# A four-layer decoder trunk on one Trainium2 core: later turns, own banks, a twelfth warming product, one division for a pair of heads

## The chip, the cores and the metric

The kernel runs on one core of one Trainium2 chip. The metric is the time of one execution in device microseconds; three runs of the kernel before gave a median of 1155.39 us. The core has five engines, each with its own queue of instructions: TensorE (PE in the profile; its weight loads are shown apart as PEld), VectorE (DVE), ScalarE (ACT), GpSimd (POOL) and SyncE (SP), which here issues the DMAs. An instruction starts when those ahead of it on its engine are issued and the semaphores that it waits for are up.

## What is computed

One sequence of 256 tokens, 1024 wide, goes through four layers. Each is a token mixer behind an RMS norm, added to the residual stream, and a squared-ReLU MLP (4096 wide) behind another norm. The mixers are differential attention (layers 0 and 3), MoBA block attention (layer 1, one block of 256 here, so plain causal attention) and sliding-window attention with attention sinks (SWA, layer 2). Cut to what matters here:

```python
x = x + mixer[i % 3](rms_norm(x, g_mix), ...)
x = x + relu(rms_norm(x, g_mlp) @ w_up) ** 2 @ w_down
# diff (8 heads, value width 128):  p = softmax(q0 k0) - lam * softmax(q1 k1)
#                                   o = rms_norm(p @ v, sub_g) * (1 - lambda_init)
# MoBA and SWA (16 heads of 64):    p = exp(s - m) / l ;  o = p @ v
# SWA: only the last 128 keys count, and l = sum(exp(s - m)) + exp(sink - m)
out = rms_norm(x, final_g)
```

Products are to have float32 accuracy. The kernel splits each operand in two parts (hi and lo, type fp32r) and adds three products: hi with hi, hi with lo, lo with hi.

## The kernel before

**Weights.** The weights come as pieces of 1 MB. SP's queue fetches them five ahead (`fetch`, L57 to L69, into `raw`), ACT makes the hi part (`whi`, L80) and DVE the lo part (`wlo`, L81), two pieces ahead of their use. This goes on all the time beside everything else that ACT and DVE do.

**Layout.** The residual stream lies transposed in four tiles `hT` of 128x512. Projections (`proj`, tile `p_in`, L296) take 24 products for each of the two tiles of 128 tokens, 512 columns wide, or 256 in SWA (two pairs of heads); between the two halves of 24, the steps named `midway` are issued. The output projection (`p_d`, L271 to L273 in `mm3`) adds to four PSUM banks held through the whole of it.

**Order.** The kernel text is written as one stream; a scheduler then orders the instructions of each engine, keeping close to the text and to what is ready. Two sets of four PSUM banks rotate: "wk" (p_s0, p_s1, p_t, p_av, p_qk, p_o and the like) and "acc" (p_in, p_d, p_down, p_last). A tile that gets a bank waits for the last reader of the tile that had it.

**Heads of 64 (MoBA, SWA).** `head_block` (L415) handles two heads at once, as a generator with three steps. First `scores` (L313): TensorE makes p_s0 and p_s1, DVE adds the mask and takes the minimum of the negated scores (L333), ACT exponentiates (L336) and sums the row into `l`; SWA adds the sink's term (L340, L341). Then the division: DVE makes the reciprocal (L420) and multiplies head 0 with two tensor_scalars (L426), ACT does head 1 with two copies with a scale (L424). Second `transposed` (L346): TensorE transposes the numerators `e` (three p_t for each head, L351), ACT copies them out (`et`, L352). Third the products with the values, p_av (L434), for the two heads in one bank, each in its own 64 columns of TensorE, and the copies out as hi and lo (`oo`, L437 and L438).

In SWA, `step` (L443) keeps up to three such blocks in flight: a new block is appended, then every block in the line is given its next step, second-oldest first up to the newest, and the oldest last when there are more than three. There are four projections (`for c in range(4)`) with two blocks each; the first of them starts with p_qk, the transposes of the queries (L459), and `put_q` (`qhl`, L468 and L469). MoBA and the diff layers follow a plan written out by hand (L567 to L574): for each half of a projection a list of steps, QK (turned queries and keys), SC (scores), TR (transposed), AV (values), OUT (results).

**Diff layers.** `diff_pair` (L391) takes two heads: the values' products, the norm of each head (a reciprocal root `ry`), `o` on DVE (L404), four transposes p_o on TensorE (L409), and `oo` as hi on ACT (L411) and lo on DVE (L412). OUT(g) is the step that issues p_o and what follows for pair g. OUT(1) stands with TR(4) and AV(4) between the two halves of a projection; OUT(3) is the last step of the plan, and `out_proj_all` (L627) comes after it: four groups g of weights, eight blocks d of the output, six products for each, and group g needs `oo` of pair g.

**The tail.** `down_out` (L691) makes the last MLP's second product the other way round (p_last, tokens on the partitions), for two halves c of 512 columns and two tiles t of 128 tokens. `close` (L699) adds a bank to the residual with DVE (L702) and squares it with ACT (L704, the sum goes to `fss`); `finish` (L706) makes the reciprocal root (L710 to L717), scales the first half with ACT (L719) and the second with DVE (L722), and sends the result out. The very last tile's columns are made in two halves of 256 that share a bank: the first half is closed, then the second.

**The start.** WARM (L31) products of a tile of ones (p_warm, L133) run before the first data are there.

## Time and profile before

| | us |
|---|---|
| median of three runs (lowest, highest) | 1155.39 (1154.45, 1156.26) |
| the profiled execution, its own time | 1154.87 |
| its span, from the first to the last instruction | 1152.8 |
| of that the MoBA mixer's stretch, 308 to 421 | 113.0 |
| the SWA mixer's stretch, 600.86 to 671.83 | 70.97 |
| from the start of the last product (1145.27) to the end of the span | 7.5 |

The mean granted clock of TensorE is 0.998. The profile's groups give an instruction's line, engine, operation, output and inputs with their shapes, how often it occurs, its busy time and mean length in ns, and the idle time ahead of it with what ended it. Rows in order of time give the start, the length, the instruction, how many alike follow each other ("x4"), and in brackets how long the engine stood idle ahead of it and who released it. TensorE's products overlap, so the length of one is more than its distance to the next.

### The profile page before, as it was taken

The numbers are of one execution on the slowest core, as the hardware profiler recorded it, in microseconds if no ns is written. First come the engines' busy times: TensorE is split into PE (matmuls) and PEld (weight loads), VectorE is DVE, ScalarE is ACT, GpSimd is POOL, SyncE is SP. The second block draws the span as 40 slices with busy tenths as digits, with TensorE's granted clock in tenths as the row PEclk, the third lists the DMA queues.
The fourth block names the chain that finished last, engine by engine and source line by source line (L and its number), as shares of the span: only waits on it lengthen the run. The fifth ranks groups of instructions, "written<-read, shape, count | busy, mean of one in ns | idle before, by whom it ended". The sixth has DMA issues, their size and how long they took to land.

```text
span 1152.8 us, 17102 instructions
## 1 busy us (share of the span) xinstructions
PE 1140.4 (99%) x6558; PEld 986.6 (86%) x6558; DVE 824.3 (72%) x1631; ACT 671.6 (58%) x1239; POOL 11.4 (1%) x39
## 2 busy tenths in 40 slices
PE   9999999999999999999999999999999999999997
PEld 7789888888887888888898888888888889888886
DVE  8978977656666698775568787775567788777453
ACT  6866655544476765654447866654447676665342
POOL 1000000000000000000000000000000000000000
PEclk9999999999999999999999999999999999999999
DMA  8543455555544355555564246555553434554551
GB/s 327 194 146 119 160 200 193 199 190 183 183 146 145 116 178 193 200 192 183 185 209 142 74 147 206 195 184 186 184 201 129 152 136 155 194 199 166 186 179 36
DMA packets 30608, 198.66 MB, mean 172 GB/s; under 512 B 3520, under 2 KB 5184, under 8 KB 7360
## 3 DMA queue, kind: packets, MB, share of 16 engines
q1 hardware_dynamic: 30240, 197.06, 49.6%
q8 instruction: 51, 0.84, 0.3%
q10 hardware_dynamic: 288, 0.52, 0.1%
q14 instruction: 29, 0.24, 0.1%
HBM read 196.52 MB, written 1.05 MB: 171 GB/s over the span
## 4 chain that ended last, share of the span: by engine, by line
PE 92%; DVE 3%; ACT 2%; DMA 2%; issue 1%; SPq 0%; DVEq 0%; ACTq 0%
PE p_up L603 20%; PE p_in L296 16%; PE p_down L603 15%; PE p_up L604 10%; PE p_down L604 8%; PE p_last L271 2%; PE p_last L273 2%; PE p_last L272 2%; PE p_d L273 2%; PE p_d L271 2%; DMA raw<-in_weights 2%; PE p_d L272 2%; PE p_av L434 1%; PE p_t L351 1%; PE p_s L271 1%; PE p_qk L459 1%
## 5 line engine op out<-in xcount | busy, mean ns | idle before, releaser
L81 DVE TENSOR_TENSOR wlo<-raw,whi 128x1024 fp32r<-128x1024 f32 (+1 forms) x374 | 447.1, 1209 | 202.9 <-ACT whi L80 201.9
L80 ACT ACTIVATE whi<-raw 128x1024 fp32r<-128x1024 f32 (+1 forms) x374 | 384.7, 1045 | 210.1 <-issue 111.1
L603 PE MATMUL p_up<-hg,whi 128*128 128x512 f32 x1024 | 356.9, 393 | 0.5 <-DVE hg L229 0.2
L604 PE MATMUL p_up<-hg,wlo 128*128 128x256 f32 x1024 | 284.9, 279 | 0.0
L603 PE MATMUL p_down<-uu,whi 128*128 128x512 f32 x768 | 266.4, 392 | 0.0
L603 PEld LDWEIGHTS p_up<-hg,whi 128*128 128x128 f32 x1024 | 191.5, 187 | 43.3 <-DVE hg L229 0.7
L604 PE MATMUL p_down<-uu,wlo 128*128 128x256 f32 x768 | 214.3, 279 | 0.0
L296 PE MATMUL p_in<-whi,hg 128*128 128x512 f32 (+1 forms) x736 | 212.9, 372 | 0.1
L604 PEld LDWEIGHTS p_up<-hg,wlo 128*128 128x128 f32 x1024 | 193.2, 189 | 0.5
L603 PEld LDWEIGHTS p_down<-uu,whi 128*128 128x128 f32 x768 | 143.7, 187 | 32.1
L296 PEld LDWEIGHTS p_in<-whi,hg 128*128 128x128 f32 x736 | 131.8, 188 | 24.7 <-issue 1.2
L604 PEld LDWEIGHTS p_down<-uu,wlo 128*128 128x128 f32 x768 | 144.8, 189 | 0.0
L296 PE MATMUL p_in<-wlo,hg 128*128 128x512 f32 (+1 forms) x368 | 130.3, 368 | 0.1
L676 ACT ACTIVATE uu<-u 128x512 fp32r<-128x512 f32 x64 | 40.5, 633 | 70.9 <-DVE u L674 70.9
L296 PEld LDWEIGHTS p_in<-wlo,hg 128*128 128x128 f32 x368 | 68.8, 188 | 12.1 <-DVE wlo L81 1.3
L609 ACT ACTIVATE cross<-p_up 128x256 f32<-128x256 f32 x128 | 48.1, 376 | 39.4 <-PE p_up L604 34.0
L228 ACT ACTIVATE hg<-hT,gn 128x256 fp32r<-128x256 f32 x64 | 31.6, 503 | 65.6 <-DVE hT L622 65.1
L336 ACT ACTIVATE e<-ns,nm 128x128 f32<-128x128 f32 (+1 forms) x128 | 56.8, 447 | 10.3 <-DVE nm L333 10.0
L677 DVE TENSOR_TENSOR uu<-u,uu 128x512 fp32r<-128x512 f32 x64 | 44.2, 691 | 21.5 <-ACT uu L676 21.5
L271 PE MATMUL p_d<-oo,whi 128*128 128x256 f32 x192 | 56.2, 293 | 0.0
L272 PE MATMUL p_d<-oo,whi 128*128 128x256 f32 x192 | 55.1, 287 | 0.0
L273 PE MATMUL p_d<-oo,wlo 128*128 128x256 f32 x192 | 54.7, 288 | 0.0
(182 smaller groups left out, 1262.1 us busy)
## 6 DMA issues: line engine op xcount, KB each, us to landing
raw<-in_weights SPq DMA_DIRECT2D x181, 1024.0 KB, 4.8
raw<-in_weights SPq DMA_DIRECT2D x8, 256.0 KB, 4.6
raw<-in_weights SPq DMA_DIRECT2D x4, 512.0 KB, 7.6
hT<-in_xT SPq DMA_DIRECT2D x8, 128.0 KB, 4.5
bias<-in_swa_row SPq DMA_DIRECT2D x1, 512.0 KB, 3.6
grow<-in_fng SPq DMA_DIRECT2D x1, 512.0 KB, 3.5
out<-res SPq DMA_DIRECT2D x4, 128.0 KB, 2.1
out<-res ACTq DMA_DIRECT2D x2, 256.0 KB, 2.2
```

The costliest lines, as they stand in the source:

```text
L80: A.activation(hi[:, s], raw[:, s], AF.Copy)
L81: V.tensor_tensor(lo[:, s], raw[:, s], f(hi[:, s]), op=OP.subtract)
L271: T.matmul(out, lh, rh, start=start, stop=False, **kw)
L272: T.matmul(out, lh, rl, start=False, stop=False, **kw)
L273: T.matmul(out, ll, rh, start=False, stop=stop, **kw)
L296: T.matmul(out[t], n.both[k // 2][:, k % 2, x, P * t:P * t + P], r3(kb)(parts[k // kb][w])[:, k % kb, :], start=fresh, stop=k == 7 and x + ...
L336: A.activation(e[:, s], ns[:, s], AF.Exp, bias=nm[:, t:t + 1], scale=-1.0, accum_out=l[:, t:t + 1])
L603: T.matmul(r3(2)(p), hi, x, start=start, stop=False, skip_group_check=True)
L604: T.matmul(p[:, :S], lo, x[:, 0], start=False, stop=stop, skip_group_check=True)
L609: A.activation(cross, p[:, S:], AF.Copy)
L676: A.activation(both[:, :, 0], r3(2)(u), AF.Copy)
L677: V.tensor_tensor(both[:, :, 1], r3(2)(u), f(both[:, :, 0]), op=OP.subtract)
```

## The change

- WARM goes from 11 to 12.
- `scores` keeps the two heads' row sums in one tile `ls`, and the sink's terms in one tile `es`, added at once for both heads.
- `head_block` makes the reciprocals for both heads (one of 128x4, one more of 128x2 for the third block of columns) and divides both with one DVE multiplication of 128x768 (L427 of the new kernel). The two tensor_scalars and the two ACT copies go.
- `transposed` takes head 1 first, then head 0.
- `step` gives the newest block its step first, then the older ones; the oldest, which ends, is last.
- In the diff layers OUT(1) moves from between the halves of a projection to after the second half, ahead of TR(5); OUT(3) moves into `out_proj_all`, to group 2, block 4. For MoBA and SWA the new argument `rest` does nothing.
- In `down_out` the last piece's products (q = 7) of the last two halves go to banks of their own; what came before (q up to 6) is closed 512 columns wide, without a square, and two closes of 256 follow. The tiles `nw` get seven buffers instead of six.

```diff
@@ -28,7 +28,7 @@
 NEG = -1.0e38
 LOOK = 2
 FAR = 5
-WARM = 11
+WARM = 12
 RAW = 4
 
 
@@ -203,7 +203,7 @@
 
     def rsqrt(y, x, n):
 
-        t = tiny.tile([P, n], F32, tag="nw", name="nw", bufs=6)
+        t = tiny.tile([P, n], F32, tag="nw", name="nw", bufs=7)
         V.tensor_scalar(y.bitcast(I32), x.bitcast(I32), -0.5, 1597463007.0, op0=OP.mult, op1=OP.add)
         for _ in range(3):
             V.tensor_tensor(t, y, y, op=OP.mult)
@@ -320,12 +320,15 @@
             a = slice(P * t, P * t + P)
             mm3(o, qh[:, a], ql[:, a], kh[:, :, :n], kl[:, :, :n], True, True)
         out = []
+        if sinks is not None:
+            es = tiny.tile([P, 2 * NT], F32, tag="es", name="es", bufs=2)
         scored[0] += 1
         pair_e = room(4 + scored[0] % 2, [P, 2, 3 * P], "e")
+        ls = tiny.tile([P, 2 * NT], F32, tag="l", name="l", bufs=5)
         for c in range(2):
             ns = sb.tile([P, 3 * P], F32, tag="ns", name="ns", bufs=2)
             nm = tiny.tile([P, NT], F32, tag="nm", name="nm", bufs=4)
-            l = tiny.tile([P, NT], F32, tag="l", name="l", bufs=6)
+            l = ls[:, NT * c:NT * c + NT]
             e = pair_e[:, c]
             mk = mask[:, :, :].rearrange("p a b -> p (a b)")
             for t, p, n in ((0, p0, P), (1, p1, S)):
@@ -336,16 +339,16 @@
                 A.activation(e[:, s], ns[:, s], AF.Exp, bias=nm[:, t:t + 1], scale=-1.0,
                              accum_out=l[:, t:t + 1])
             if sinks is not None:
-                es = tiny.tile([P, NT], F32, tag="es", name="es", bufs=2)
-                A.activation(es, nm, AF.Exp, bias=sinks[c][0])
-                V.tensor_tensor(l, l, es, op=OP.add)
+                A.activation(es[:, NT * c:NT * c + NT], nm, AF.Exp, bias=sinks[c][0])
             out.append((e, l))
-        return out
+        if sinks is not None:
+            V.tensor_tensor(ls, ls, es, op=OP.add)
+        return out, pair_e, ls
 
     def transposed(es):
         turned[0] += 1
         ts = room((6, 7, 12, 13)[turned[0] % 4], [P, 2, 3 * P], "et")
-        for i, e in enumerate(es):
+        for i, e in reversed(list(enumerate(es))):
             p = bank("wk", "p_t")
             for j in range(3):
                 T.transpose(p[:, P * j:P * j + P], e[:, P * j:P * j + P], ident)
@@ -376,7 +379,7 @@
 
     def diff_head(slot, q, k, el):
 
-        e, l = zip(*scores(q, k, causal, None))
+        e, l = zip(*scores(q, k, causal, None)[0])
         c2 = tiny.tile([P, NT], F32, tag="c2", name="c2")
         V.reciprocal(c2, l[1])
         V.scalar_tensor_tensor(c2, c2, nlam[:, slot:slot + 1], l[0], op0=OP.mult, op1=OP.mult)
@@ -414,16 +417,15 @@
 
     def head_block(parts, q, k, v, mask, sinks, b):
 
-        rl = tiny.tile([P, NT, 2], F32, tag="rl2", name="rl2")
-        es, ls = zip(*scores(q, k, mask, sinks))
-        for c in range(2):
-            V.reciprocal(rl[:, :, c], ls[c])
-            for t in range(NT):
-                s = slice(0, P) if t == 0 else slice(P, 3 * P)
-                if c:
-                    A.activation(es[c][:, s], es[c][:, s], AF.Copy, scale=rl[:, t, c:c + 1])
-                else:
-                    V.tensor_scalar(es[c][:, s], es[c][:, s], rl[:, t, c:c + 1], None, op0=OP.mult)
+        _, both_e, l = scores(q, k, mask, sinks)
+
+        rl = tiny.tile([P, 2, 3], F32, tag="rl3", name="rl3")
+        l = l.rearrange("p (c t) -> p c t", c=2)
+        V.reciprocal(rl[:, :, 0:2], l)
+        V.reciprocal(rl[:, :, 2:3], l[:, :, 1:2])
+        e = both_e.rearrange("p c (j m) -> p c j m", j=3)
+        V.tensor_tensor(e, e, rl[:, :, :, None].to_broadcast([P, 2, 3, P]), op=OP.mult)
+        es = [both_e[:, c] for c in range(2)]
         yield
         ets = transposed(es)
         yield
@@ -444,7 +446,7 @@
 
         line.append(block)
         full = len(line) > 3
-        for x in line[full:] + line[:full]:
+        for x in line[:0:-1] + line[:1] if full else line[::-1]:
             if x is not None:
                 next(x, None)
         if full:
@@ -569,9 +571,9 @@
                     [(TR, 4), (QK, 3), (OUT, 1), (SC, 6)], [(TR, 5), (SC, 7)],
                     [(AV, 4), (TR, 6), (AV, 5), (TR, 7), (AV, 6), (OUT, 2), (AV, 7), (OUT, 3)]]
             if mixer == 0:
-                plan[8:] = [[(AV, 2), (QK, 2), (OUT, 0), (SC, 4)], [(AV, 3), (SC, 5)], [(TR, 4), (AV, 4), (OUT, 1)],
-                            [(TR, 5), (AV, 5)],
-                            [(QK, 3), (SC, 6), (SC, 7), (OUT, 2), (TR, 6), (AV, 6), (TR, 7), (AV, 7), (OUT, 3)]]
+                plan[8:] = [[(AV, 2), (QK, 2), (OUT, 0), (SC, 4)], [(AV, 3), (SC, 5)], [(TR, 4), (AV, 4)],
+                            [(OUT, 1), (TR, 5), (AV, 5)],
+                            [(QK, 3), (SC, 6), (SC, 7), (OUT, 2), (TR, 6), (AV, 6), (TR, 7), (AV, 7)]]
             for at, c in enumerate(order):
                 p = proj(n, (512, 2), at == 0, [lambda do=do, x=x: do(x) for do, x in plan[2 * at]])
                 if i == 0 and at == 0:
@@ -589,13 +591,13 @@
                     do(x)
             for do, x in plan[-1]:
                 do(x)
-            return parts
+            return parts, (lambda: OUT(3))
         for do in first + second:
             do()
         for _ in range(3):
             step()
         line.clear()
-        return parts
+        return parts, lambda: None
 
 
 
@@ -624,12 +626,14 @@
         if b:
             norm_sum(n, j)
 
-    def out_proj_all(parts, n):
+    def out_proj_all(parts, n, rest):
 
         banks = [bank("acc", f"p_d{j}") for j in range(4)]
         for g in range(4):
             hi, lo = (r3(2)(x) for x in take())
             for d in range(8):
+                if (g, d) == (2, 4):
+                    rest()
                 p = banks[d // 2][:, S * (d % 2):S * (d % 2) + S]
                 w = slice(P * d, P * d + P)
                 for a in range(2):
@@ -639,7 +643,7 @@
                 if g == 3:
                     into(n, d, p, None, True)
 
-    def out_proj(parts, n):
+    def out_proj(parts, n, rest):
 
         banks = [bank("acc", f"p_d{j}") for j in range(4)]
         two = [[r3(4)(x) for x in take()] for _ in range(2)]
@@ -696,19 +700,21 @@
         x = cst.tile([P, 2, NT], F32, name="fx")
         r = cst.tile([P, NT], F32, name="fr")
 
-        def close(t, bank, c, part, first, width):
-
+        def close(t, p, c, part, first=0):
+
+            width = p.shape[-1]
             y = res[t][:, 512 * c + first:512 * c + first + width]
-            V.scalar_tensor_tensor(y, bank[:, first:first + width], factor[:, t:t + 1], y, op0=OP.mult, op1=OP.add)
-            sq = sb.tile([P, 512], F32, tag="relu", name="sq")
-            A.activation(sq[:, :width], y, AF.Square, accum_out=ss[:, part, t:t + 1])
+            V.scalar_tensor_tensor(y, p, factor[:, t:t + 1], y, op0=OP.mult, op1=OP.add)
+            if part is not None:
+                sq = sb.tile([P, 512], F32, tag="relu", name="sq")
+                A.activation(sq[:, :width], y, AF.Square, accum_out=ss[:, part, t:t + 1])
 
         def finish(t, halves):
 
             o = slice(t, t + 1)
             last = x[:, 1, o]
             V.scalar_tensor_tensor(last, ss[:, halves, o], 0.5 / D, x[:, 0, o], op0=OP.mult, op1=OP.add)
-            y, w = r[:, o], tiny.tile([P, 1], F32, tag="nw", name="nw", bufs=6)
+            y, w = r[:, o], tiny.tile([P, 1], F32, tag="nw", name="nw", bufs=7)
 
             V.tensor_scalar(y.bitcast(I32), last.bitcast(I32), -0.5, 1597463007.0 - 2.0 ** 22 - 2.0 ** 31,
                             op0=OP.mult, op1=OP.add)
@@ -732,12 +738,15 @@
             banks = [bank("acc", "p_last") for _ in range(NT)]
             parts = []
 
-            def last(t, ks, cols=slice(0, 512)):
+            def last(t, ks, p=None, first=0, alone=False):
+                p = banks[t] if p is None else p
+                cols = slice(first, first + p.shape[-1])
                 for q, k in ks:
                     hi, lo = parts[q]
                     u, s = us[4 * q + k], slice(P * t, P * t + P)
-                    mm3(banks[t][:, cols], u[:, 0, s], u[:, 1, s], hi[:, k, cols], lo[:, k, cols],
-                        q + k == 0, q + k == 10, skip_group_check=True)
+                    mm3(p, u[:, 0, s], u[:, 1, s], hi[:, k, cols], lo[:, k, cols],
+                        (q, k) == (ks[0] if alone else (0, 0)), (q, k) == ks[-1] and k == 3 and q > 5,
+                        skip_group_check=True)
 
             for q in range(8):
                 parts.append([r3(4)(x) for x in take()])
@@ -747,20 +756,23 @@
                             last(t, [(q, k)])
             ends = [(q, k) for q in (6, 7) for k in range(4)]
             last(0, ends)
-            close(0, banks[0], c, c, 0, 512)
+            close(0, banks[0], c, c)
             if c == 0:
                 last(1, ends)
-                close(1, banks[1], 0, 0, 0, 512)
+                close(1, banks[1], 0, 0)
                 for t in range(NT):
                     y = res[t][:, :512]
                     V.tensor_tensor(y, y, grow[:, :512], op=OP.mult)
                     sofar(t, [])
             else:
                 finish(0, 1)
+
                 last(1, ends[:4])
+                close(1, banks[1], 1, None)
                 for h in range(2):
-                    last(1, ends[4:], slice(256 * h, 256 * h + 256))
-                    close(1, banks[1], 1, 1 + h, 256 * h, 256)
+                    p = bank("acc", "p_last")[:, :256]
+                    last(1, ends[4:], p, 256 * h, True)
+                    close(1, p, 1, 1 + h, 256 * h)
                     if h == 0:
                         sofar(1, [1])
                 finish(1, 2)
@@ -774,9 +786,9 @@
     for j in range(4):
         norm_sum(n, j)
     for i in range(DEPTH):
-        parts = mixer_layer(i, n)
+        parts, rest = mixer_layer(i, n)
         n = new_norm(gv[:, 1, i, :])
-        (out_proj if i % 3 == 1 else out_proj_all)(parts, n)
+        (out_proj if i % 3 == 1 else out_proj_all)(parts, n, rest)
         held = {}
 
         def then(g):
```

## The prediction

> **What bounds the kernel now.** I read the page first, then TensorE's waits, then a table of stages, then rows in order of time at the places that the diff touches.
>
> ```profile
> PE 1140.4 (99%) x6558; PEld 986.6 (86%) x6558; DVE 824.3 (72%) x1631; ACT 671.6 (58%) x1239; POOL 11.4 (1%) x39
> ...
> PE 92%; DVE 3%; ACT 2%; DMA 2%; issue 1%; SPq 0%; DVEq 0%; ACTq 0%
> ```
>
> TensorE is busy for 99% of the span and carries 92% of the chain that ended last. No other engine sets the whole; a gain must shorten TensorE's own row of products, or the little after its last one. Busy time of TensorE hides things, though, since its products overlap: a 512-wide product is recorded as 0.39 us long, and the next starts 0.23 us after it. So I count from start to start. The steady distances come from two rows:
>
> ```profile
> 88.31 0.62 PE L296 MATMUL p_in<-whi,hg 128*128 128x512 f32 x2
> ```
>
> ```profile
> 629.25 0.40 PE L296 MATMUL p_in<-whi,hg 128*128 128x256 f32 x2
> ```
>
> Two 512-wide products take 0.62, one 0.39, so the distance is 0.23; for 256 columns it is 0.40 - 0.28 = 0.12 (a lone 0.39 and 0.28 stand in rows further down). What exceeds these is loss.
>
> Two stages of layers with heads of 64 and the waits (columns of the first fence: us waited, times, longest; of the second: stretch, its length, busy time and count on PE, PEld, DVE, ACT, POOL, then clock, DMA share, GB/s):
>
> ```profile
> PE p_o L409 <- DVE o L404: 1.5, 4, 0.5
> ```
>
> ```profile
> 600.86:671.83 70.97, 70.67 (x540) 62.23 (x539) 54.63 (x194) 50.52 (x143) 0.00 (x0) 1.00 0.32 109
> 633.00:645.40 12.40, 12.40 (x94) 10.47 (x93) 9.70 (x42) 10.60 (x34) 0.00 (x0) 1.00 0.26 88
> ```
>
> The first row of stages is the whole SWA mixer, the second one projection of it with its two pairs of heads. The clock is 1.00, so no term below comes from a changed clock.
>
> **The change, part by part.** The sum is made against the profiled execution's own time, 1154.87 us; the median of the runs shown, 1155.39, is 0.5 above it.
>
> *SWA layer, order of turns.* TensorE computes p_av for two heads of 64, each in half of its columns. Where the products of both heads stand next to each other, they run side by side:
>
> ```profile
> 621.31 0.87 PE L434 MATMUL p_av<-et,rest 128*64 128x256 f32 x8
> 622.11 0.39 PE L296 MATMUL p_in<-whi,hg 128*128 128x256 f32 x1
> ```
>
> ```profile
> 626.63 0.65 PE L434 MATMUL p_av<-et,rest 128*64 128x256 f32 x2
> 627.21 0.39 PE L296 MATMUL p_in<-whi,hg 128*128 128x256 f32 x1
> ...
> 627.64 0.86 PE L434 MATMUL p_av<-et,rest 128*64 128x256 f32 x6
> 628.43 0.50 PE L296 MATMUL p_in<-whi,hg 128*128 128x256 f32 x2
> ```
>
> ```profile
> 662.91 0.65 PE L434 MATMUL p_av<-et,rest 128*64 128x256 f32 x2
> ```
>
> The eight records of one pair take 622.11 - 621.31 = 0.80 us together. In the second fence head 1's transposed numerators come late, head 0's first product goes alone, two p_in fill the gap, and the pair takes 628.43 - 626.63 = 1.80, less 0.24 for the two p_in, which is 1.56. A split pair thus costs 0.76 more. It happens four times (626.63 is the first, 662.91 the last). In the order of the changed kernel all eight pairs stand unsplit, because the newest pair is given out first and head 1 is transposed ahead of head 0. That is worth 4 x 0.76 = 3.0 us. Gathering the p_t (the diff also makes runs of six out of scattered ones) I cost at nothing:
>
> ```profile
> 636.59 0.29 PE L272 MATMUL p_d<-oo,whi 128*128 128x256 f32 x1
> ...
> 637.28 0.28 PE L272 MATMUL p_d<-oo,whi 128*128 128x256 f32 x1
> ```
>
> Between these two starts TensorE does three p_d and three p_t, scattered, in 0.69: less 3 x 0.12 that is 0.11 for a p_t, as in the run of three in the fence on the diff layers ((0.49 - 0.27) / 2, where 0.27 is one alone).
>
> Against this stand two waits that the new order brings in the second pair of each projection: p_av needs a bank that ACT's copy et of the p_t group just before it must empty, with only the other p_t group and two p_in between, and the second p_t group needs the bank that DVE's oo empties, which is queued on DVE right behind the new multiplication. Behind the waiting TensorE instruction stands everything else, p_qk first. The view of groups in the SWA stretch gives the lengths:
>
> ```profile
> L81 DVE TENSOR_TENSOR wlo<-raw,whi 128x1024 fp32r<-128x1024 f32 x16 | 19.4, 1216 | 2.1 <-ACT whi L80 2.1
> ...
> L352 ACT ACTIVATE et<-p_t 128x384 f32<-128x384 f32 x16 | 7.7, 483 | 5.3 <-PE p_t L351 5.3
> ...
> L426 DVE TENSOR_SCALAR e<-e,rl 128x256 f32<-128x256 f32 x8 | 2.8, 347 | 0.0
> ...
> L426 DVE TENSOR_SCALAR e<-e,rl 128x128 f32<-128x128 f32 x8 | 2.3, 282 | 0.1
> ```
>
> The copy is 0.48 us long and TensorE has some 0.5 of work beside it; a wait of 0.1 to 0.4 for one pair is my estimate, and the bounds are nothing and 0.76, which eats the gain. I take 0.25 for four pairs, 1.0. **SWA: -3.0 + 1.0 = -2.0.**
>
> *The division.* Per pair, DVE gives up two tensor_scalars (0.35 + 0.28, which overlap by about 0.1 as such neighbours do in the timeline, so 0.54) and ACT two copies; DVE gets one multiplication of 768 columns. A TENSOR_TENSOR of 1024 columns takes 1.22 (row above), one of 512 takes 0.69 (L404, next fence), so 768 should take 0.95, and DVE has 0.41 more per pair. Two pairs in a projection: 9.70 + 0.82 = 10.5 busy of about 11.9. It still fits beside TensorE, so I cost it at nothing apart from the waits above; with the cover gone it would show whole (third rival). From 128 to 256 columns the tensor_scalar grew by 65 ns, from 512 to 1024 the TENSOR_TENSOR by 527: 0.5 and 1.0 ns a column. [...]
>
> MoBA uses the same division, but its pairs are not split before and its order moves by three p_in only. I take 0, bounds -0.5 and +0.8 (eight pairs, a wait of 0.1 each).
>
> *Diff layers, OUT(1) and OUT(3).* Rows of layer 0 (in brackets: idle time ahead and its releaser):
>
> ```profile
> 84.24 0.69 DVE L404 TENSOR_TENSOR o<-p_av,ry 128x512 f32<-128x512 f32 x1
> 84.45 0.39 PE L296 MATMUL p_in<-wlo,hg 128*128 128x512 f32 x1
> 85.08 0.63 PE L409 MATMUL p_o<-ident,o 128*128 128x128 f32 x4 [0.24 <-DVE o L404]
> 85.74 0.69 ACT L411 ACTIVATE oo<-p_o,gn 128x512 fp32r<-128x512 f32 x1 [1.28 <-PE p_o L409]
> ...
> 90.10 0.69 ACT L586 ACTIVATE qk<-p_in,nr 128x512 f32<-128x512 f32 x1 [0.72 <-PE p_in L296]
> 90.68 0.48 ACT L352 ACTIVATE et<-p_t 128x384 f32<-128x384 f32 x1
> 90.81 0.36 PE L271 MATMUL p_d<-oo,whi 128*128 128x256 f32 x1
> 91.22 0.49 PE L357 MATMUL p_av<-v,et 128*128 128x128 f32 x2
> ...
> 109.98 0.28 PE L272 MATMUL p_d<-oo,whi 128*128 128x256 f32 x1
> 110.78 0.63 PE L409 MATMUL p_o<-ident,o 128*128 128x128 f32 x4 [0.52 <-DVE o L404]
> ```
>
> The first p_o starts 0.63 after the product ahead of it instead of 0.23: 0.40 lost. The last one starts 0.80 after, instead of 0.12: 0.68 lost. After the change OUT(3) stands 24 products of p_d (24 x 0.12 = 2.9 us, less those already ahead of it: about 2.2 later) further on, so o is long there; the next 2.9 us of p_d hide ACT's and DVE's oo. That gains the 0.68. OUT(1) comes after all 24 p_in of its half, long after its o. Its ACT copy oo (0.69) now stands between qk and et on ACT, so et comes about 0.6 later, while TensorE arrives 0.4 later for the four p_o in front: at 91.22, where p_av already waits 0.2 for et, I add 0.1. DVE's oo also enters the rope, whose p_qk was just in time. Per layer -0.68 - 0.40 + 0.1 = -1.0, in two such layers **-2.0**; bounds -0.7 and -1.1 per layer (an OUT(1) that gains nothing; nothing late).
>
> *The tail.*
>
> ```profile
> 1139.17 0.75 DVE L702 SCALAR_TENSOR_TENSOR res<-p_last,factor,res 128x512 f32<-128x512 f32 x1 [7.43 <-PE p_last L273]
> ...
> 1142.24 0.16 DVE L717 SCALAR_TENSOR_TENSOR fr<-nw,fr 128x1 f32<-128x1 f32 x1
> 1142.43 0.88 DVE L722 SCALAR_TENSOR_TENSOR res<-res,fr,grow 128x256 f32<-128x256 f32 x2
> 1143.00 0.28 PE L273 MATMUL p_last<-whi,uu 128*128 128x256 f32 x1
> 1143.32 0.48 DVE L702 SCALAR_TENSOR_TENSOR res<-p_last,factor,res 128x256 f32<-128x256 f32 x1
> 1143.85 0.39 PE L271 MATMUL p_last<-whi,uu 128*128 128x256 f32 x1 [0.58 <-DVE res L702]
> ...
> 1145.58 0.48 DVE L702 SCALAR_TENSOR_TENSOR res<-p_last,factor,res 128x256 f32<-128x256 f32 x1 [1.05 <-PE p_last L273]
> ```
>
> The second half waits until DVE has closed the first one in the same bank: 1143.85 - 1143.00 - 0.12 = 0.73 lost. With own banks that goes. DVE pays a further 512-wide close (0.75), which goes in ahead of L717: 1142.24 to 1143.0, then L717 and the two L722 to 1144.1, the first close to 1144.6, and the second half has left TensorE by 1145.58 - 0.73 = 1144.8. The last close starts there, 0.7 to 0.8 earlier; the extra 512-wide one is hidden in DVE's idle 1.05. **-0.7**; bounds 0 and -0.8.
>
> *The twelfth warming product.*
>
> ```profile
> 1.00 4.58 PE L133 MATMUL p_warm<-ones 128*128 128x128 f32 x22 [1.00 <-POOL ones L124]
> 5.68 1.45 PE L296 MATMUL p_in<-whi,hg 128*128 128x512 f32 x4
> ```
>
> The 22 records (two a product) end at 5.58; p_in starts at 5.68, when ACT's hg is there. Two more at about 0.11 end at about the same moment: 0, at worst +0.1.
>
> **Sum:** -2.0 - 2.0 - 0.7 = -4.7, from 1154.87 to 1150.2; with the median as the base it would be 1150.7. I take 1150.3.
>
> **The rivals.**
>
> *No new waits* (0.16). TensorE's work and ACT's freed time cover both new waits: -3.0 - 2.2 - 0.8 = -6.0, 1148.9. For it speaks ACT, which has its two divisions a pair less; against it, the bank that is refilled half a microsecond after its use.
>
> *The bank waits eat the SWA gain* (0.16). Each of the four pairs waits 0.76: SWA 0, sum -2.7, 1152.2. For it speaks that oo stands behind the long multiplication on DVE.
>
> *The change does not do what it says* (0.13). The p_o waits come back as waits of p_t for et and of p_qk for the rope, and the SWA pairs wait as well: only the tail stays, -0.7, 1154.2. Against it stands the 2.2 us of other products in front of OUT(3).
>
> *DVE sets the pace* (0.07), the one on the slower side. Before, TensorE could transpose head 0 after 0.54 us of DVE while ACT divided head 1; now no p_t of a pair starts until the whole 0.95 is done. If TensorE reaches p_t when the multiplication is only starting, it loses 0.95 in each of 16 pairs of MoBA and SWA: 15.2 - 5.7 (the gains of SWA without waits, diff and tail) = +9.5, 1164.4. It decides from 0.36 us a pair on (5.7 / 16). [...] Against it:
>
> ```profile
> 632.40 0.35 DVE L333 CUSTOM_DVE_ANT_0 ns<-p_s,band,rest 128x128 f32<-128x128 f32 x1 [1.61 <-PE p_s L273]
> ```
>
> DVE stood idle for 1.61 us here until TensorE came with p_s, four times the 0.41 that a pair adds.
>
> **How the numbers follow.** The forecast (1150.3) has 0.48. Measurements of this kernel can tell about 0.2% from no change, 2.3 us: faster means below 1153.1, slower above 1157.7. Forecast, no new waits and eaten gain are all faster (0.80), the fourth is the same (0.13), DVE's pace is slower (0.07). The range leaves out the last and most of the fourth: from 1147.9 (every term at its good bound, -6.5, less 0.5 for the spread of the runs, 1154.45 to 1156.26) to 1153.4 (diff at -1.4 and tail at -0.7 with nothing from SWA, plus 0.6 for that spread and the base).
>
> **What would show it.** All eight p_av groups of SWA unsplit, 0.8 us each; rows of p_av waiting for et or p_t for oo, 0.1 to 0.4 long; no p_o line in TensorE's waits, and p_last's wait for res gone with the last close near 1140.5 to 1141; a 768-wide multiplication of 0.95. It would be wrong if TensorE waits for e in the SWA or MoBA stretch, if the SWA stretch stays near 70.97, or if the p_t behind OUT(1) are late.

## The result, and the profile after

The changed kernel takes 1148.49 us (median of six runs, 1148.08 to 1149.48) against 1154.86 for the kernel before (six runs, 1154.45 to 1156.26): ratio 0.9946, with a 95% interval of 0.9935 to 0.9956. That is 6.4 us faster; the forecast was 1150.3, with a range of 1147.9 to 1153.4. The profiled execution took 1148.08 us, its span is 1146.0.

First the page of the changed kernel: busy time by engine, and the chain that ended last.

```profile
PE 1135.6 (99%) x6560; PEld 988.2 (86%) x6560; DVE 827.8 (72%) x1608; ACT 660.0 (58%) x1207; POOL 11.4 (1%) x39
...
PE 95%; DVE 2%; DMA 1%; ACT 1%; issue 0%; SPq 0%; DVEq 0%; ACTq 0%
```

TensorE has two records more (the twelfth warming product) and is still busy for 99%. DVE has 3.5 us more, ACT 11.6 less: the division changed engines. Of the 6.8 us by which the span shrank, 4.8 had been recorded as busy time of TensorE; that is what the prediction meant by busy time that hides things, and why it counted from start to start.

All of TensorE's waits of 0.2 us and more in the changed kernel (us in total, times, longest):

```profile
PE p_warm L133 <- POOL ones L124: 1.0, 1, 1.0
PE p_qk L461 <- DVE qk L309: 0.7, 1, 0.7
PE p_s L271 <- issue: 0.6, 1, 0.6
PE p_up L605 <- DVE hg L229: 0.2, 1, 0.2
```

The line p_o <- DVE o and the line p_last <- DVE res are gone, and none has come in their place.

Where the time went is best read from the lengths of the stages, each from its first product to the first of the next stage. The two rows of the view of stages for SWA, before and after (stretch, length, then busy time and count of PE, PEld, DVE, ACT, POOL, clock, DMA share, GB/s):

```profile
593.57:671.83 78.26, 77.96 (x598) 69.32 (x597) 59.69 (x202) 54.69 (x148) 0.00 (x0) 1.00 0.35 120
```

```profile
591.82:667.11 75.29, 74.95 (x599) 69.01 (x597) 60.81 (x187) 48.27 (x132) 0.00 (x0) 1.00 0.37 125
```

All five stages that the diff touches, in us, for both kernels and for the twelve of the experiments (layer 0 with the start, from 0 to the first p_up; MoBA, SWA and layer 3 from the first p_in to the first p_up; the tail from the first p_last to the end):

| kernel | layer 0 | MoBA | SWA | layer 3 | tail |
|---|---|---|---|---|---|
| before | 120.46 | 114.66 | 78.27 | 111.88 | 95.43 |
| changed | 119.24 | 114.24 | 75.29 | 110.74 | 94.61 |
| e1 before + reversed heads | 120.77 | 115.03 | 75.81 | 111.94 | 95.44 |
| e2 before + new step order | 120.29 | 114.71 | 76.97 | 111.94 | 95.44 |
| e3 changed, heads not reversed | 119.22 | 114.54 | 75.34 | 110.70 | 94.61 |
| e4 changed, old division | 119.48 | 114.96 | 75.86 | 110.69 | 94.61 |
| e5 changed, p_av head by head | 119.22 | 114.67 | 75.32 | 110.80 | 94.61 |
| e6 changed, two multiplications | 119.47 | 114.64 | 80.47 | 110.73 | 94.60 |
| e7 changed, old step order | 119.40 | 114.58 | 80.76 | 110.71 | 94.60 |
| e8 changed, old tail | 119.44 | 114.57 | 75.27 | 110.72 | 95.43 |
| e9 changed, old OUT(1) | 120.24 | 114.29 | 75.27 | 111.20 | 94.61 |
| e10 changed, old OUT(3) | 120.19 | 114.58 | 75.25 | 111.48 | 94.61 |
| e11 changed, eleven warming products | 119.37 | 114.63 | 75.29 | 110.77 | 94.61 |
| e12 e5 + a transpose between heads | 119.32 | 122.21 | 82.70 | 110.71 | 94.63 |

Where nothing was changed, SWA, layer 3 and the tail repeat within 0.1 us, MoBA within 0.4 (114.24 to 114.63 for the same MoBA in the changed kernel and e7 to e11) and layer 0 within 0.5 (120.28 to 120.78 for the same layer 0 in the kernel before, e1 and e2). So differences in SWA, layer 3 and the tail are read from one profile, with one exception (SWA in e6, see there); the 0.42 us of MoBA are not shown to be an effect at all. The intervals of whole times are wider, 0.2 to 0.3% from end to end.

The change by stages: SWA -2.98, layer 0 -1.22, layer 3 -1.14, tail -0.82, MoBA -0.42 (within its spread), the MLPs between -0.15; in all -6.7.

TensorE in the changed kernel, in order of time, at one of the SWA pairs for which the prediction feared a wait:

```profile
627.04 0.82 PE L354 MATMUL p_t<-ident,e 128*128 128x128 f32 x6
627.61 0.48 PE L296 MATMUL p_in<-whi,hg 128*128 128x256 f32 x2
628.11 0.87 PE L436 MATMUL p_av<-et,rest 128*64 128x256 f32 x8
628.91 0.66 PE L461 MATMUL p_qk<-ident,qn 128*128 128x128 f32 x4
```

and DVE just before it, with the new multiplication:

```profile
625.80 0.95 DVE L427 TENSOR_TENSOR e<-e,rl 128x768 f32<-128x768 f32 x1
626.67 0.42 DVE L440 TENSOR_TENSOR oo<-p_av,oo 128x256 fp32r<-128x256 f32 x1
```

The six p_t come in a run, the eight p_av records too, in 0.80 us (628.91 - 628.11). The multiplication took 0.95, as interpolated, and ended at 626.75, 0.29 ahead of the first p_t. Over the eight pairs of SWA that distance is 0.26 to 0.92 us. TensorE never waits there.

OUT(1) and OUT(3) in layer 0 of the changed kernel:

```profile
88.70 0.39 PE L296 MATMUL p_in<-whi,hg 128*128 128x512 f32 x1
88.93 0.60 PE L412 MATMUL p_o<-ident,o 128*128 128x128 f32 x4
89.37 0.49 PE L354 MATMUL p_t<-ident,e 128*128 128x128 f32 x3
```

```profile
111.75 0.28 PE L273 MATMUL p_d<-oo,wlo 128*128 128x256 f32 x1
111.87 0.60 PE L412 MATMUL p_o<-ident,o 128*128 128x128 f32 x4
```

Both p_o start at the steady distance, 0.23 and 0.12, after the product ahead. At OUT(1) ACT then has three things in a row, the new et last:

```profile
89.13 0.69 ACT L588 ACTIVATE qk<-p_in,nr 128x512 f32<-128x512 f32 x1 [0.71 <-PE p_in L296]
89.72 0.68 ACT L414 ACTIVATE oo<-p_o,gn 128x512 fp32r<-128x512 f32 x1
90.29 0.49 ACT L355 ACTIVATE et<-p_t 128x384 f32<-128x384 f32 x1
```

The p_av that needs this et starts at 90.83, with two p_d drawn in ahead of it instead of one.

The tail, DVE's closes and the two products where the second half begins:

```profile
1136.24 0.74 DVE L707 SCALAR_TENSOR_TENSOR res<-p_last,factor,res 128x512 f32<-128x512 f32 x1
...
1137.88 0.48 DVE L707 SCALAR_TENSOR_TENSOR res<-p_last,factor,res 128x256 f32<-128x256 f32 x1
1138.86 0.48 DVE L707 SCALAR_TENSOR_TENSOR res<-p_last,factor,res 128x256 f32<-128x256 f32 x1 [0.50 <-PE p_last L273]
```

```profile
1137.11 0.28 PE L273 MATMUL p_last<-whi,uu 128*128 128x256 f32 x1
1137.23 0.28 PE L271 MATMUL p_last<-whi,uu 128*128 128x256 f32 x1
```

TensorE goes from the first half to the second in 0.12 us. DVE still stands idle for 0.50 ahead of the last close, so the extra close (0.74) is hidden as worked out.

### The profile page after: what moved, and what is told of

Same layout as the page of the kernel before. It is cut to its first block, busy times and chain, and to the rows that moved or that the text cites. A ratio compares the mean times of both kernels' runs of the same rounds, so it can differ in the third digit from the quotient of the medians.

```text
span 1146.0 us, 17054 instructions
## 1 busy us (share of the span) xinstructions
PE 1135.6 (99%) x6560; PEld 988.2 (86%) x6560; DVE 827.8 (72%) x1608; ACT 660.0 (58%) x1207; POOL 11.4 (1%) x39
## 4 chain that ended last, share of the span: by engine, by line
PE 95%; DVE 2%; DMA 1%; ACT 1%; issue 0%; SPq 0%; DVEq 0%; ACTq 0%
PE p_up L605 20%; PE p_in L296 18%; PE p_down L605 15%; PE p_up L606 11%; PE p_down L606 8%; PE p_last L272 3%; PE p_last L271 3%; PE p_last L273 3%; PE p_d L272 2%; PE p_d L273 2%; PE p_d L271 2%; DMA raw<-in_weights 1%; PE p_t L354 1%; PE p_s L271 1%; PE p_qk L461 1%; PE p_av L436 1%
## 5 line engine op out<-in xcount | busy, mean ns | idle before, releaser
L339 ACT ACTIVATE e<-ns,nm 128x128 f32<-128x128 f32 (+1 forms) x128 | 56.8, 446 | 11.6 <-DVE nm L336 11.2
L612 DVE TENSOR_TENSOR relu<-p_up,cross 128x256 f32<-128x256 f32 x128 | 53.6, 419 | 1.5 <-ACT cross L611 1.5
```

What stands on the lines that cost most here:

```text
L339: A.activation(e[:, s], ns[:, s], AF.Exp, bias=nm[:, t:t + 1], scale=-1.0, accum_out=l[:, t:t + 1])
L612: V.tensor_tensor(out, p[:, :S], cross, op=OP.add)
```

## The experiments

Theory: SWA gains because the two heads' p_av products, each in 64 of TensorE's columns, run side by side in all eight pairs instead of four; the gains of the diff layers and of the tail are the waits that were taken away. Rivals: the later turns gain by themselves; the new division gains (ACT's freed time) or costs (DVE's longer work). "Split" means that products of another kind stand between the two heads' p_av.

**e1: the kernel before with head 1 transposed first.**

```diff
-        for i, e in enumerate(es):
+        for i, e in reversed(list(enumerate(es))):
```

> The kernel before with one edit: head 1 is transposed ahead of head 0; step's order, the division, the plan of the diff layers and the tail stay. In the order of the instructions all eight p_av groups of SWA then stand unsplit. Theory (the SWA layer gains because the two heads' p_av products run side by side again, 0.76 us for each of four pairs): the SWA mixer, 78.3 us from its first p_in to the first p_up before and 75.3 in the changed kernel, comes to about 75.4, and the whole is 2.9 us (0.25%) faster. Rival (the gain is that of later turns: TensorE no longer stands between the two heads' p_t): without the new step order nothing is gained, SWA 78.3. Rival (the division's two lost ACT copies make et early): also 78.3.

Measured 1152.76 us, ratio to before 0.9982 (0.9973 to 0.9991), 2.35 us faster; SWA 75.81, -2.46. With one line and no later turn most of SWA's gain is there. No p_av is split in it; the p_t are gathered too, apart from one pair. Two things keep it from the 3.0 of four split pairs: its last pair takes 1.17 although nothing stands between its records (663.99 to 665.16; the second head's first product starts 0.38 behind the first head's), and TensorE waits 0.6 instead of 0.2 for hg ahead of the first p_up.

**e2: the kernel before with the newest pair given out first.**

```diff
-        for x in line[full:] + line[:full]:
+        for x in line[:0:-1] + line[:1] if full else line[::-1]:
```

> The kernel before with one edit: step gives the newest block its turn first. In the order of the instructions three of the eight p_av groups of SWA are still split. Theory (split pairs at 0.76 us): one split less, SWA 77.5 us, the whole 0.8 us faster. Rival (later turns are what gains, by gathering p_t and p_s): SWA about 75.3 to 76, the whole 2 to 3 us faster.

Measured 1153.49 us, 0.9987 (0.9977 to 0.9996), 1.6 us faster; SWA 76.97, -1.30: between the two. A split pair of it, with p_t between:

```profile
629.15 0.65 PE L434 MATMUL p_av<-et,rest 128*64 128x256 f32 x2
629.72 0.44 PE L351 MATMUL p_t<-ident,e 128*128 128x128 f32 x2
630.09 0.86 PE L434 MATMUL p_av<-et,rest 128*64 128x256 f32 x6
630.89 0.33 PE L459 MATMUL p_qk<-ident,qn 128*128 128x128 f32 x1
```

From 629.15 to 630.89 it takes 1.74 us, less 0.22 for two p_t, 1.52 against 0.80: 0.72 lost. A second pair loses the same, and the last two pairs, of which one is split, lose 0.57 together (653.72 to 656.11, less 0.22 and twice 0.80). That is 2.0 us against 3.0 before, so the split pairs explain 1.0 of the 1.30. The other 0.3 belongs to the order itself or to other waits of it; it was not taken apart.

**e3: the changed kernel, heads in the old order.**

```diff
-        for i, e in reversed(list(enumerate(es))):
+        for i, e in enumerate(es):
```

> The changed kernel with head 0 transposed first again. In the order of the instructions no p_av group of SWA is split, since both heads' numerators come out of one multiplication. Theory (split pairs): SWA stays at 75.3 within 0.3, no difference from the changed kernel. Rival (the reversal is what pays): SWA back to about 78.

Measured 1148.44 us, 0.9944 (0.9928 to 0.9961); SWA 75.34. No difference: with one multiplication for both heads, both come ready at once, and the reversal has nothing left to do.

**e4: the changed kernel with the old division.**

```diff
-        V.reciprocal(rl[:, :, 0:2], l)
...
-        V.tensor_tensor(e, e, rl[:, :, :, None].to_broadcast([P, 2, 3, P]), op=OP.mult)
+        for c in range(2):
+            V.reciprocal(rl[:, :, c], ls[c])
...
+                if c:
+                    A.activation(es[c][:, s], es[c][:, s], AF.Copy, scale=rl[:, t, c:c + 1])
+                else:
+                    V.tensor_scalar(es[c][:, s], es[c][:, s], rl[:, t, c:c + 1], None, op0=OP.mult)
```

> The changed kernel with the division of before in MoBA and SWA (head 0 by two tensor_scalars on DVE, head 1 by two copies on ACT). In the order of the instructions one p_av group of SWA is split. Theory (split pairs): SWA 75.3 + 0.8 = 76.1, MoBA as before the change (114.7 us from first p_in to first p_up) or as after it (114.2), which tells where those 0.4 come from; the whole about 1 us slower than the changed kernel. Rival (the one multiplication costs TensorE time, 0.41 us of DVE a pair): this kernel is faster than the changed one by up to a few us.

Measured 1149.64 us, 0.9954 (0.9939 to 0.9969), 1.15 slower than the changed kernel; SWA 75.86, +0.57, with one split pair (it loses 0.72). MoBA is 114.96. With the old division it takes 114.66 to 115.03 (before, e1, e2, e4), with one new multiplication 114.24 to 114.67 (e12 aside); with a spread of 0.4 that is a hint that the division helps there, not more.

**e5: p_av head by head.**

```diff
-        for m, cols in ((0, slice(0, S)), (1, slice(P, S))):
-            for c in range(2):
+        for c in range(2):
+            for m, cols in ((0, slice(0, S)), (1, slice(P, S))):
```

> The changed kernel with p_av in another order: all of head 0's products of a pair, then all of head 1's, in MoBA and SWA (16 pairs); the sums are the same. Theory (products of different 64 columns of TensorE run side by side only when they are neighbours): the eight records of a pair take 0.80 us together now and about 1.35 then (0.27 + 0.21 for the two 256-wide ones of a head, 0.21 for its two 128-wide ones, twice), +0.55 for each of 16 pairs, about +9 us, half of it in SWA. Rival (a split pair cost what it did because of the change from one kind of product to another): the pairs stay unsplit here, so no difference.

Measured 1149.01 us, 0.9952 (0.9937 to 0.9966), 0.5 slower than the changed kernel, which lies in MoBA and inside its spread; SWA 75.32, the same. The theory as it was put there fell: products need not be neighbours.

```profile
628.56 0.88 PE L436 MATMUL p_av<-et,rest 128*64 128x256 f32 x8
629.37 0.33 PE L461 MATMUL p_qk<-ident,qn 128*128 128x128 f32 x1
```

Eight records in 0.81 us in this order as well. Either TensorE overlaps the heads across two instructions, or the price of a split pair had come from something else. e12 tells these apart.

**e12: e5 with a transpose of all 128 columns between the heads.** It goes to an unused part of the same bank.

```diff
         for c in range(2):
+            if c:
+                T.transpose(p[:, S:S + P], ets[1][:, 0:P], ident)
             for m, cols in ((0, slice(0, S)), (1, slice(P, S))):
```

> The kernel of the head-by-head run with one transpose of 128 columns (all 128 columns of TensorE) put between head 0's and head 1's products of every pair, into an unused part of the same bank; nobody reads it. In the head-by-head run the records of the two heads still started 13 ns apart, and nothing was lost. Theory (products of different 64 columns run side by side though others of their kind stand between, but not across a product that uses all columns): each of 16 pairs loses the 0.11 us of the transpose and 0.55 to 0.76 of overlap, +10.6 to +14 us against the changed kernel, 75.3 to about 81 us in SWA. Rival (a split pair lost its time in another way, by waits): 0.11 for each of 16 pairs, +1.8 us, SWA 76.2.

Measured 1163.60 us, ratio to before 1.0076 (1.0059 to 1.0092), 15.1 us above the changed kernel; SWA +7.4, MoBA +8.0, on average 0.96 for each pair.

```profile
631.50 0.86 PE L438 MATMUL p_av<-et,rest 128*64 128x256 f32 x4
632.30 0.33 PE L435 MATMUL p_av<-ident,et 128*128 128x128 f32 x1
632.56 0.86 PE L438 MATMUL p_av<-et,rest 128*64 128x256 f32 x4
633.35 0.39 PE L271 MATMUL p_s<-kpadh,qhl 128*128 128x256 f32 x1
```

Head 0 alone takes 0.80 us, head 1 alone 0.79: each as long as both together above. TensorE waits for nobody in this stretch. The pair takes 1.85 (633.35 - 631.50) instead of 0.80. So the second head is free as long as no product that uses all columns stands between the heads (and, by the last pair of e1, as long as its numerators are there in time), and what runs alone is lost if one does. The two heads need not even be of one pair: at the end of SWA nothing stands between the second head of the seventh pair and the first head of the eighth, and these eight records take 0.81 (669.64 to 670.45).

The split pairs of before had p_in or p_d between. In the one that the prediction shows, only head 0's first product went alone, for 0.58 (627.21 - 626.63); the two p_in took 0.43 instead of 0.24, and the other six records 0.79. So about 0.57 of the 0.76 is the product that ran alone, and 0.19 lies in going over to full-width products and back: the first p_in behind a p_av takes 0.22 to the next start, and p_av starts 0.20 or more behind the p_in ahead of it, where the steady distance is 0.12.

**e6: the multiplication twice** (the second by ones, in place).

```diff
         V.tensor_tensor(e, e, rl[:, :, :, None].to_broadcast([P, 2, 3, P]), op=OP.mult)
+        V.tensor_tensor(e, e, ones[:, None, None, :].to_broadcast([P, 2, 3, P]), op=OP.mult)
```

> The changed kernel with the division's multiplication followed by a second one of the same size in place, by a tile of ones: 0.95 us more of DVE and 0.95 us later numerators in each of 16 pairs; the values are unchanged. In the changed kernel TensorE's p_t starts 0.3 to 0.9 us after the end of its multiplication in the eight pairs of SWA, and 0.15 to several us after it in MoBA. Theory (the multiplication is hidden, with that much slack): TensorE loses 0.95 less the slack, 3.2 us over SWA and about 1 in MoBA, +4 us with 2 to 7 as bounds. Rival (DVE sets the pace): the whole 15 us. Rival (DVE has much to spare): under 1 us.

Measured 1152.09 us, 0.9979 (0.9969 to 0.9988), 3.6 above the changed kernel. MoBA (114.64) has room for a second multiplication at no cost that shows; SWA (80.47) has not. The profiled execution is the slowest of the ten (1153.93 us, its span 5.9 above the changed kernel's), and its +5.2 in SWA holds more than the multiplication: from 636.8 to 640.1 the granted clock was 0.50, and p_d products started 0.21 us apart instead of 0.12. An estimate from these 3.3 us at half the clock is 1.7 us lost. The waits that are new in this profile, 2.7 us in SWA, are not at p_t:

```profile
PE p_d L271 <- ACT oo L440: 2.3, 3, 1.6
...
PE p_d L272 <- DVE oo L441: 0.4, 1, 0.4
```

Numerators that come later delay the pair's results, and TensorE stands at the output projection's p_d. The rest of the 5.2, about 0.8, was not taken apart.

**e7: the changed kernel with step's old order.** (The edit of e2, undone.)

> The changed kernel with step's order of before (second-oldest block first). In the order of the instructions all eight p_av groups of SWA are unsplit. Theory (split pairs): SWA 75.3 within 0.4, so the later turns by themselves are worth nothing measurable. Rival (later turns gain by themselves): SWA 76 to 78.

Measured 1152.94 us, 0.9983 (0.9974 to 0.9993), 4.45 above the changed kernel; SWA +5.5, of which 1.2 comes back in the MLP behind it (twelve of the p_d that the changed kernel makes behind its first p_up stand ahead of it here). All pairs are unsplit, and yet SWA is 2.5 us slower than before the change (80.76 against 78.27): here the theory fell short. Its waits:

```profile
PE p_d L271 <- ACT oo L439: 2.1, 4, 0.6
```

```profile
666.47 0.82 PE L354 MATMUL p_t<-ident,e 128*128 128x128 f32 x6
667.92 0.87 PE L436 MATMUL p_av<-et,rest 128*64 128x256 f32 x8 [0.63 <-ACT et L355]
669.27 0.74 PE L271 MATMUL p_d<-oo,whi 128*128 128x256 f32 x4 [0.48 <-ACT oo L439]
```

At the end of the layer p_t, et, p_av, oo and p_d now follow each other with nothing between, and p_d waits for oo three times earlier too. These waits are 2.7 of the 5.5. With the old division the old order did not cost this. Side by side, all with head 1 transposed first: old division and old order 75.81 (e1), old division and new order 75.86 (e4), new division and old order 80.76, both new 75.29. So the later turns are what makes room for the one long multiplication, and the two together bring 0.5 beyond e1's one line; by themselves (e2) the later turns bring part of the unsplit pairs.

**e8: the changed kernel with the old tail.**

```diff
-                last(1, ends[:4])
-                close(1, banks[1], 1, None)
...
-                    p = bank("acc", "p_last")[:, :256]
-                    last(1, ends[4:], p, 256 * h, True)
+                    last(1, ends[4:], slice(256 * h, 256 * h + 256))
```

> The changed kernel with the last halves in one bank as before. Theory (the wait for the close is 0.73 us of TensorE, and the extra close of 512 columns is hidden): +0.8 us, the stretch from the first p_last to the end 95.4 instead of 94.6 us. Rival (the extra close delays the end as much as the wait did): no difference.

Measured 1149.29 us, 0.9953 (0.9938 to 0.9968), 0.8 above the changed kernel; tail 95.43 against 94.61. As the theory had it.

**e9 and e10: one OUT step each put back.**

```diff
-                ... [(TR, 4), (AV, 4)],
-                            [(OUT, 1), (TR, 5), (AV, 5)],
+                ... [(TR, 4), (AV, 4), (OUT, 1)],
+                            [(TR, 5), (AV, 5)],
```

> The changed kernel with OUT(1) between the two halves of the projection again, OUT(3) inside out_proj_all as changed. Theory (p_o waited 0.40 us for o on DVE, and the move costs 0.1 by a later et): TensorE's wait for p_o comes back once in each diff layer, +0.3 us a layer, +0.6 us in all. Rival (the wait for et takes the place of the one removed): no difference.

```diff
-                            ... (TR, 7), (AV, 7)]]
+                            ... (TR, 7), (AV, 7), (OUT, 3)]]
...
-            return parts, (lambda: OUT(3))
+            return parts, lambda: None
```

> The changed kernel with OUT(3) ahead of out_proj_all again, OUT(1) as changed. Theory: p_o waits 0.68 us in each diff layer, +1.4 us in all. Rival (the products of group 3 wait for oo in the changed kernel): no difference.

Measured 1149.49 us, 0.9951 (0.9937 to 0.9966), and 1150.09 us, 0.9957 (0.9940 to 0.9974): 1.0 and 1.6 above the changed kernel. Layer 3 shows them cleanly: +0.46 and +0.74, together 1.20 against the 1.14 that the layer had gained. The waits are back, here that of OUT(1) in layer 0 and that of OUT(3) in layer 3:

```profile
85.57 0.63 PE L412 MATMUL p_o<-ident,o 128*128 128x128 f32 x4 [0.24 <-DVE o L407]
```

```profile
950.66 0.63 PE L412 MATMUL p_o<-ident,o 128*128 128x128 f32 x4 [0.53 <-DVE o L407]
```

In layer 0 each shows +0.9 to +1.0; in e9 0.56 of that is there already at the p_t ahead of the moved step (83.68 against 83.12), so part of it is the start, which differs from one execution to the next. The whole times, 1.0 and 1.6, are about twice what layer 3 shows, as for two layers alike.

**e11: the changed kernel with eleven warming products** (WARM = 11).

> The changed kernel with eleven warming products. In the profile of the changed kernel the warming products ran at 0.213 us until 5.9 us and the first p_in started at 6.03, 0.35 later than before, but the first p_in then took 0.23 to 0.31 us instead of 0.34 to 0.39, and the 13th stood 0.2 us earlier than before. Theory (the twelfth product is worth nothing; when the granted speed steps up differs from run to run): the whole within 0.3 us of the changed kernel. Rival (the twelfth keeps TensorE busy until p_in and so keeps it at speed): +0.2 to +0.5 us.

Measured 1148.70 us, 0.9945 (0.9930 to 0.9960), 0.2 above; layer 0 119.37 against 119.24. Both inside the spread of the start: the twelfth product is worth nothing that shows.

No experiment pointed to a version that beats the changed kernel; e3 shows that one of its lines can be left out. The row sums kept in one tile (`ls`, `es`) were not tried apart; they stand in e4 as well.

## Why the prediction was right

The sum was -4.7 and the profiled executions differ by 6.8. Of the 2.1 between them 1.0 lies in SWA, 0.4 in the diff layers, 0.1 in the tail, and 0.6 in MoBA and the MLPs, which the sum put at nothing and where no effect is shown. SWA, the diff layers and the tail gained by the mechanisms that were forecast; half of the difference is one term, the second below. The measured 1148.49 lies near the low end of the range, which took every term at its good bound. Step by step:

- **SWA, split pairs, -3.0.** Measured -2.98 for the whole stage. The cause, side-by-side products, is shown by e12, though e5 corrects it: not neighbours, but no full-width product between. The price of a split pair, 0.76, also fits the split pairs of e2 (0.72, 0.72, 0.57) and e4 (0.72; the stage +0.57).
- **SWA, the two new waits, +1.0.** The step that was mis-sized. In the rows of the changed kernel shown above, the second p_in starts at 627.81 (627.61 + 0.48 - 0.28) and p_av 0.30 later. At a first pair of a projection, which has no such wait, it is 0.20:

```profile
623.21 0.28 PE L296 MATMUL p_in<-whi,hg 128*128 128x256 f32 x1
623.41 0.87 PE L436 MATMUL p_av<-et,rest 128*64 128x256 f32 x8
```

So the wait is 0.1 at two of the four pairs, nothing at the others, and nothing for oo. It is the wait that was named: this p_av starts 0.05 after ACT's first et has ended (627.57 + 0.49 = 628.06). That ACT empties the bank in time because it no longer divides in between is only argued. So it was the rival without new waits, 1148.9 with a chance of 0.16, that came true; the forecast's 0.25 a pair was an estimate, and it was too high.
- **The division at nothing.** Right, with 0.26 to 0.92 us of room in each SWA pair. e6 shows that the room ends before a further 0.95, and e7 that it exists only with the later turns. The prediction credited the order with unsplit pairs alone; that it also hides the multiplication was missed.
- **p_t gathered, at nothing.** Not refuted, and not separated from e2's 0.3. The run of three p_t from which the prediction takes 0.11 is not in its fence on the diff layers (the 0.49 there is of two p_av); it is this row of before, just ahead of them, with the same length:

```profile
89.90 0.49 PE L351 MATMUL p_t<-ident,e 128*128 128x128 f32 x3
```

- **MoBA at nothing.** -0.42 in one profile, inside the spread of 0.4.
- **Diff layers, -2.0.** -1.14 in layer 3 and about as much in layer 0; by e9 and e10 0.46 for OUT(1), forecast 0.3, and 0.74 for OUT(3), forecast 0.68. The added wait for et did not come: one more p_d fills the gap.
- **Tail, -0.7.** -0.82 by the profiles and by e8. The last close starts at 1138.86, ahead of the 1140.5 to 1141 that was named as a sign, because the stages ahead gained more than the sum had.
- **Warming at nothing.** Right by e11, though p_in started 0.35 later; see the last section.
- **DVE sets the pace.** Not in the changed kernel. In e6 and e7, where late results do hold TensorE up, the place is not the one that the prediction named: TensorE stood at p_d for oo and at p_av for et, not at p_t for e.

## What to carry to other kernels

When TensorE is busy for 99%, look for loss in the distances between starts: a product that used half of the columns alone, with a full-width one behind it, is busy time that could have been shared (in e12 one head alone took 0.80 us, as long as both heads take together in the changed kernel). Two changes that gain little or even lose alone can need each other: here a long DVE instruction was free only after its reader had been moved back (without that, in e7, SWA took 5.5 us more), so undo the parts of such a change one by one before judging any of them. Try the smallest part alone as well: one line (e1) brought 2.46 of SWA's 2.98. And ask of a late result not only its first reader, but the last one in the chain: the late numerators of e6 showed up as a wait of 2.3 us for oo.

## What the runs showed of the hardware

TensorE's warming did not take the same time in each execution. The first two rows of TensorE in the changed kernel:

```profile
1.00 5.27 PE L133 MATMUL p_warm<-ones 128*128 128x128 f32 x24 [1.00 <-POOL ones L124]
6.03 1.17 PE L296 MATMUL p_in<-whi,hg 128*128 128x512 f32 x4
```

A warming record starts 0.21 us after the one ahead of it (the second 0.37) until some moment, and 0.11 afterwards. With the first record always at 1.0, the first short distance begins between 3.9 and 5.9 us in ten of the fourteen profiles; in the other four (e3, e4, e7, e12) all 24 records keep 0.21, up to the last at 6.07. The first p_in starts at 5.50 to 5.68 in the four profiles with eleven warming products and at 5.66 to 6.14 in the ten with twelve. By the 25th p_in nothing of that is left: it starts at 11.9 to 12.4 in all of them, and not earlier where the first was early (e9: 5.70 and 12.39; the changed kernel: 6.03 and 11.89).

Once the clock fell in the middle of the kernel. In the profile of e6 it was granted at 0.50 from 636.8 to 640.1; 1.2 us earlier TensorE had ended a wait of 1.64 us for oo, the longest of all waits in these profiles. Whether the wait is the cause is not shown: it happened once, and no other profile has such a wait or such a fall.
